# A two-layer decoder step on one core: layer 0's weight casts move from VectorE to ScalarE

## The chip, the core and the metric

One NeuronCore of a Trainium2 chip runs the whole program. Its engines are TensorE (PE in the profile; PEld is its weight load), VectorE (DVE), ScalarE (ACT), GpSimd (POOL) and SyncE (SP), whose queue issues the transfers. Each engine works off its own instructions in order. The metric is the device time of one execution in microseconds; it is the median of three runs, and lower is better.

## What is computed

```python
# layer 0: gated linear attention (GLA), 4 heads, key width 128, value width 256, chunks of 64
h = rms_norm(x, norm_gain[0])              # x: 1024 prompt rows, and 8 x 8 sample rows
u = h @ w_in                               # q, k, v, gate and a code of rank 16, in one projection
log_a = log_sigmoid(a_code @ w_up + b_a) / 16
# per chunk: b = cumsum(log_a); qd = q*exp(b); kd = k*exp(-b)
#   o = qd @ S + tril(qd @ kd^T) @ v;   S = S*exp(b_last) + (k*exp(b_last - b))^T @ v
x = x + (rms_norm(o, onorm) * silu(g)) @ w_out
# layer 1: stick-breaking attention with a paged cache for the samples, the same frame around it
```

`rms_norm(x, gain) = x * rsqrt(mean(x*x) + 1e-6) * gain`. The gain of layer 0 is not multiplied into the rows of x: it is multiplied into the rows of `w_in`, as the weights are prepared.

## The kernel before, in words

**Two-part numbers.** TensorE multiplies numbers of a reduced type (`F32R`). Each fp32 operand is held as a high part (`hi`, the number cast to that type) and a low part (`lo`, the number less its high part), and a product is three matmuls: hi·hi, hi·lo, lo·hi. So each weight tile, raw 128 x 512 in fp32 (`wr`), is prepared by `split` into `whi` and `wlo`. Layer 0's input weights are multiplied by the norm's vector (`gain`, one number for each partition) ahead of that.

**Weight tiles.** They are numbered n in the order of their use. n = 0 is the weight of the code. Then each head has four tiles for q and k (each holds two 128-row blocks, so two gains of 256 columns each) and eight for v and gate (one gain of 512 columns each): n = 1 to 12 for head 0, 13 to 24 for head 1, up to 48. From n = 49 on come weights without a gain. `place_weights` gives each tile a due time. A raw tile is fetched when the tile three before it has been split (three raw buffers), and the parts lie in a ring of ten buffers each, so a tile's parts are written when TensorE has done with the tile ten before it.

**`split` for n = 5 to 48.** VectorE multiplies the raw tile by the gain in place (L217) and casts it (L221). The low part is subtracted (L222) on VectorE where n % 3 is 2 (15 of these 44 tiles: 12 of v and gate, 3 of q and k), else on GpSimd (29 tiles). For n = 1 to 4 GpSimd multiplies (L215) and VectorE casts.

**Layer 0 by heads.** A head begins with three groups of columns of the input (c = 0, 1, 2: 384, 384 and 320 rows of x). For each, `dense_t` (L316) makes q and then k in 24 matmuls apiece; the results stand in two accumulation banks in turn. `q_out` (L497, L499) and `k_out` (L509 to L513) multiply them by the decay factors on VectorE, and so free the banks. The factors come from `decay_logits` (ScalarE L451 to L455), `decay_sums` (VectorE: xb L463, two scans L465 and L466, differences L470 and L471) and `decay_exps` (ScalarE L483 to L487). Then nine row tiles follow (`dense` L294, v and gate), with the attention of each tile (`gla_att`, `gla_state`, `gla_out`) some steps behind. The last of the nine holds the 64 sample rows; its two halves are added by `whole_rows` (ScalarE L336, then VectorE L337), and its work (L577, L578, L580, L622, L632, L635) reaches into the next head's q and k groups. This stretch, in which one head's tail and the next head's start share the engines, is called the boundary below; there are three. In head 0 the groups also hold the code (L439 to L441 take it out of its bank), and there is no older head's tail.

**What sets the order.** TensorE's order is written out by hand, as a list of times (`Timeline`). On the other engines a scheduler orders the instructions by its own simulated times when the program is built; only the gain multiplications are held in program order. A change of engine in `split` therefore moves other instructions too.

Of the kernel before, what the change touches and what calls it, by code (L numbers as in the profile page):

```python
# [13 lines left out]
AF = mybir.ActivationFunctionType  # L14
OP = mybir.AluOpType
# [61 lines left out]
def tile_hybrid_decoder(ctx, tc, x_prompt, x_sample, state_gla, cache_k, cache_v, page_table,  # L77
# [3 lines left out]
    nc = tc.nc  # L81
# [15 lines left out]
    ACT_FROM, WHI, DLO, OUT_A = 57, 6, 3, (57, 75)  # L97
# [30 lines left out]
    def sb(pool, name, shape, dtype=F32, bufs=2, tag=None):  # L128
        return pools[pool].tile(shape, dtype, name=name, tag=tag or name, bufs=bufs)
# [65 lines left out]
    def split(n, pool, engine):  # L195
        e = entries[n]
        raw, m = raws.pop(n)
        if m == NK * RANK:

            e.hi = wring.tile([128, 512], F32R, name="whi")  # L200
            nc.gpsimd.memset(e.hi.bitcast(F32), 0.0)
            x, y = (a[:, :NK * s].rearrange("p (k s) -> p k s", s=s) for a, s in ((raw, RANK), (e.hi, 48)))
            tc.keep_in_program_order(nc.vector.tensor_mul(x, x, gain[:, :NK, None].to_broadcast([128, NK, RANK])))
            nc.vector.tensor_copy(y[:, :, :RANK], x)
            nc.vector.tensor_sub(y[:, :, 32:], x, y[:, :, :RANK])
            return
        if pool is None:
            e.hi, e.lo = wring.tile([128, 512], F32R, name="whi"), wring.tile([128, 512], F32R, name="wlo")
        else:
            name, tag = pool  # L210
            e.hi, e.lo = (sb(name, f"w{i}{n}", [128, 512], F32R, 1, f"w{i}{tag}") for i in range(2))
        for s, k in e.gains:
            if 0 < n < 5:
                x = raw[:, s]
                nc.gpsimd.tensor_mul(x, x, gain[:, k:k + 1].to_broadcast(x.shape))  # L215
            else:
                tc.keep_in_program_order(nc.vector.tensor_scalar(raw[:, s], raw[:, s], gain[:, k:k + 1], None, op0=OP.mult))  # L217
        if e.first > ACT_FROM and n % 8 < WHI:
            nc.scalar.activation(e.hi[:, :m], raw[:, :m], AF.Copy)
        else:  # L220
            nc.vector.tensor_copy(e.hi[:, :m], raw[:, :m])  # L221
        engine.tensor_sub(e.lo[:, :m], raw[:, :m], e.hi[:, :m])  # L222

    def place_weights(own):

        inring, times, further = [], [], [None] * XRING
        for n, e in enumerate(entries):
            if n in own:
                pool, s = own[n]
            else:  # L230
                pool = None
                s = entries[inring[-RING]].last + 0.01 if len(inring) >= RING else e.first - (FIRST0 if n == 0 else FIRST if n < 5 else FIRST5)
                if e.first > open2 + 1 and e.last < last:
                    ends = [entries[x].last + 0.01 if x is not None else open2 + 0.01 for x in further] + [s]
                    x = ends.index(min(ends))
                    if x < XRING:
                        s, pool, further[x] = ends[x], ("at2", x), n
                if pool is None:
                    inring.append(n)
            s = max([s] + [x + 0.002 for x in times[-1:]])  # L240
            assert s < e.first - 0.05, (n, s, e.first)
            times.append(s)
            on_vector = n % 3 != 0 if OUT_A[0] < e.first < OUT_A[1] else n % 3 == 2 and DLO < e.first < 90
            at(s, split, n, pool, nc.vector if on_vector else nc.gpsimd)
            at(times[n - RAW] + 0.001 if n >= RAW else RAW0 + n * 0.01, fetch, n)
# [98 lines left out]
    gain = const.tile([128, NK], F32, name="gain")  # L344
# [318 lines left out]
    for h in range(GH):  # L663
# [3 lines left out]
        for c, (c_0, n) in enumerate(CH):  # L667
# [12 lines left out]
            for j, (key, out) in enumerate((("q", q_out), ("k", k_out))):  # L680
                lo, hi = a + (b - a) * 0.5 * j, a + (b - a) * 0.5 * (j + 1)
                dense_t(lo, hi, c_0, n, wqk,
                        lambda w, k, j=j: (w[k // 2], slice((k % 2) * 256 + j * 128, (k % 2) * 256 + j * 128 + 128)),
# [307 lines left out]
    for p in range(PAIRS):  # L991
# [27 lines left out]
        for m in range(NP // 2):  # L1019
# [20 lines left out]
            if p == PAIRS - 1:  # L1040
                st = {}
                for g in range(4):
                    n = 2 if g < 3 else 1
# [163 lines left out]
    for c, t in steps[:2 * NP - TAIL] + [(0, NP), (1, NP)] + steps[2 * NP - TAIL:]:  # L1207
# [5 lines left out]
        e = i + span  # L1213
# [41 lines left out]
```

## Time and profile before

| What | Value |
|---|---|
| median of 3 runs | 1347.07 us (1346.45 to 1347.56) |
| the profiled execution, its own time | 1348.02 us |
| its span in the profile | 1346.2 us |
| TensorE busy | 1270.1 us (94%) |
| VectorE busy | 1004.1 us (75%) |
| ScalarE busy | 719.9 us (53%) |
| GpSimd busy | 504.5 us (37%) |

The span is the time between the first and the last instruction that the profile has; the 1.8 us beside it lie before and after. Layer 0's four heads take the span's first 400 us, the output projection goes on to about 525 us, and layer 1 has the rest. A matmul's end is modelled, so TensorE's busy time overlaps from one instruction to the next; where it waits, the timeline says for what, in brackets.

### The profile page before, as it was taken

What the parts mean: (1) busy time and instruction counts of PE and PEld (TensorE: products, weight loads), DVE (VectorE), ACT (ScalarE), POOL (GpSimd) and SP (SyncE); (2) the same over time, 40 slices, a digit from 0 to 9 for tenths busy, and PEclk for the clock granted to TensorE, in tenths of its full rate; (3) what the DMA queues carried; (4) which work ended last, traced back from release to release, by engine and by line L of the source; (5) the groups of instructions that cost most, each with busy time, mean ns of one, the idle gap of its engine ahead of it and who ended that gap; (6) DMA issues with size and microseconds to landing.
All of it is one profiled execution on the core that took longest, in us unless ns stands there. A gap on an engine that the chain in (4) does not pass through costs nothing.

```text
span 1346.2 us, 23370 instructions
## 1 busy us (share of the span) xinstructions
PE 1270.1 (94%) x8025; PEld 1129.0 (84%) x8025; DVE 1004.1 (75%) x2029; ACT 719.9 (53%) x1664; POOL 504.5 (37%) x841
## 2 busy tenths in 40 slices
PE   6999999999999999989989999899998999999998
PEld 4788888888887788889989899898898988978665
DVE  7857858759565355698898988988889889896543
ACT  6446245254452135566666766667667677763221
POOL 6222323223121115363463634546446464343000
PEclk9999999999999999999999999999999999999999
DMA  6211401403337443020120200202002022134862
GB/s 199 84 43 44 135 20 55 125 20 100 122 95 236 139 136 114 20 71 26 33 74 23 71 27 28 79 23 70 28 28 77 25 76 84 33 124 153 313 207 79
DMA packets 118457, 115.80 MB, mean 86 GB/s; under 512 B 11003, under 2 KB 97923, under 8 KB 118339
## 3 DMA queue, kind: packets, MB, share of 16 engines
q1 hardware_dynamic: 118338, 114.31, 27.4%
q8 instruction: 64, 1.05, 0.3%
q14 instruction: 55, 0.44, 0.1%
HBM read 83.61 MB, written 30.67 MB: 85 GB/s over the span
## 4 chain that ended last, share of the span: by engine, by line
PE 55%; DVE 24%; ACT 8%; issue 4%; POOL 4%; DMA 3%; SPq 0%; DVEq 0%; POOLq 0%; ACTq 0%
PE acc L294 33%; PE acc L316 6%; DVE run L908 4%; PE z L882 3%; PE tr L929 2%; DVE aT L932 2%; PE o L943 2%; ACT qh L854 2%; DVE qk L811 2%; POOL rs L805 2%; DVE A L913 1%; DVE run L905 1%; DVE A L916 1%; PE o L545 1%; DVE whi L221 1%
## 5 line engine op out<-in xcount | busy, mean ns | idle before, releaser
L294 PE MATMUL acc<-whi,h 128*128 128x512 f32 (+1 forms) x1728 | 538.2, 374 | 8.5 <-DVE qk L811 6.7
L294 PEld LDWEIGHTS acc<-whi,h 128*128 128x128 f32 x1728 | 312.8, 189 | 39.7 <-ACT sh L953 3.7
L294 PE MATMUL acc<-wlo,h 128*128 128x512 f32 (+1 forms) x864 | 322.4, 373 | 1.2 <-POOL wlo L222 1.2
L316 PE MATMUL acc<-h,whi 128*128 128x256 f32 (+5 forms) x832 | 192.0, 316 | 20.4 <-DVE qk L811 10.7
L222 POOL TENSOR_TENSOR wlo<-wr,whi 128x512 fp32r<-128x512 f32 x92 | 133.2, 1451 | 132.9 <-DVE whi L221 56.5
L294 PEld LDWEIGHTS acc<-wlo,h 128*128 128x128 f32 x864 | 162.5, 188 | 18.6 <-POOL wlo L222 2.1
L316 PEld LDWEIGHTS acc<-h,whi 128*128 128x128 f32 (+2 forms) x832 | 138.6, 186 | 27.2 <-issue 10.5
L908 DVE TENSOR_TENSOR_SCAN run<-om,run 128x256 f32<-128x256 f32 x192 | 142.7, 783 | 15.9 <-ACT om L885 15.4
L931 ACT ACTIVATE aT<-tr 128x512 fp32r<-128x512 f32 (+1 forms) x160 | 88.8, 555 | 81.9 <-PE tr L929 80.0
L885 ACT ACTIVATE om<-z,bias 128x512 f32<-128x512 f32 (+1 forms) x160 | 103.0, 644 | 48.7 <-PE z L882 39.8
L316 PE MATMUL acc<-h,wlo 128*128 128x256 f32 (+2 forms) x392 | 122.9, 314 | 0.8 <-POOL wlo L222 0.8
L294 PE MATMUL acc<-w,h 128*128 128x384 f32 (+1 forms) x480 | 121.9, 365 | 0.9 <-DVE qk L811 0.9
L932 DVE TENSOR_TENSOR aT<-tr,aT 128x512 fp32r<-128x512 f32 (+1 forms) x160 | 100.8, 630 | 9.7 <-ACT aT L931 7.4
L929 PE MATMUL tr<-ident,A 128*128 128x128 f32 x576 | 90.0, 274 | 17.1 <-ACT A L886 4.8
L886 ACT ACTIVATE A<-z,bias 128x512 f32<-128x512 f32 (+1 forms) x160 | 102.3, 639 | 0.0
L943 PE MATMUL o<-aT,v 128*128 128x256 f32 (+1 forms) x640 | 98.3, 274 | 0.0
L929 PEld LDWEIGHTS tr<-ident,A 128*128 128x128 f32 x576 | 68.9, 140 | 32.8 <-ACT sq L800 9.0
L943 PEld LDWEIGHTS o<-aT,v 128*128 128x128 f32 x640 | 94.4, 188 | 1.9 <-DVE aT L932 1.2
L805 POOL TENSOR_TENSOR rs<-ms,half_exp 128x4 f32<-128x4 f32 (+1 forms) x72 | 86.7, 1204 | 19.6 <-DVE ms L803 17.1
L882 PE MATMUL z<-kc,qh 128*128 128x256 f32 x320 | 84.3, 286 | 7.1 <-DVE kc L859 7.1
L294 PEld LDWEIGHTS acc<-w,h 128*128 128x128 f32 x480 | 83.2, 189 | 6.3 <-issue 0.9
L900 POOL COPY run<-run 128x2 f32<-128x2 f32 x96 | 33.1, 345 | 134.9 <-DVE run L908 77.2
(273 smaller groups left out, 2491.7 us busy)
## 6 DMA issues: line engine op xcount, KB each, us to landing
wr<-in_w_in_b_dram SPq DMA_DIRECT2D x64, 256.0 KB, 3.0
wr<-in_w_in_a_dram SPq DMA_DIRECT2D x32, 256.0 KB, 3.1
kp<-in_cache_k_dram SPq DMA_DIRECT2D x16, 512.0 KB, 5.2
vp<-in_cache_v_dram SPq DMA_DIRECT2D x16, 512.0 KB, 5.3
o_d<-og SPq DMA_DIRECT2D x60, 128.0 KB, 1.8
x<-in_x_prompt_dram SPq DMA_DIRECT2D x8, 512.0 KB, 5.3
wr<-in_w_in_a_dram SPq DMA_DIRECT2D x32, 128.0 KB, 3.6
n<-in_state_gla_dram SPq DMA_DIRECT2D x8, 512.0 KB, 4.0
```

Source lines behind the costliest of these rows:

```text
L222: engine.tensor_sub(e.lo[:, :m], raw[:, :m], e.hi[:, :m])
L294: nc.tensor.matmul(st["ps"][:x.shape[1], :n], x, (w[k].hi if part == 0 else w[k].lo)[:, :n], start=first, stop=last)
L316: nc.tensor.matmul(st[key][:x.shape[1], :n], x, y, start=first, stop=last)
L805: nc.gpsimd.tensor_tensor(st["rs"][:n], ms[:n], half_exp[:n], op=OP.pow)
L882: nc.tensor.matmul(out, lhs, rhs, start=x == 0, stop=x == len(mm) - 1)
L885: nc.scalar.activation(u["om"][:, v0:], z[:, v0:], AF.Sigmoid, scale=-1.0, bias=K1["bias"][:, 1, hd:hd + 1])
L886: nc.scalar.activation(u["A"][:, v0:], z[:, v0:], AF.Sigmoid, bias=K1["bias"][:, 0, hd:hd + 1])
L908: nc.vector.tensor_tensor_scan(run[:, a, n - 1::-1], rev, rev, before[:, a, 0:1], op0=OP.mult, op1=OP.bypass)
L929: nc.tensor.transpose(tr[:, x], u["A"][:, col:col + 128], ident)
L931: nc.scalar.activation(hi[:, v0:], tr[:, v0:], AF.Copy)
L932: nc.vector.tensor_sub(lo[:, v0:], tr[:, v0:], hi[:, v0:])
L943: nc.tensor.matmul(q["po"][:, j, q0:], vs, part[:, x * 256 + q0:(x + 1) * 256], start=first and n == 0, stop=last and n == 3)
```

## The change

For n = 5 to 48, `split` casts on ScalarE instead of VectorE. Where the low part is VectorE's (15 tiles), the multiplication in place is gone: ScalarE multiplies by the gain as it casts (one instruction for each gain), and VectorE makes the low part in one `scalar_tensor_tensor`, raw times gain less high part. Where the low part is GpSimd's (29 tiles), VectorE still multiplies in place, then ScalarE casts, then GpSimd subtracts. The tiles n = 0 to 4 and those from 49 on are as they were.

```diff
--- before.py
+++ after.py
@@ -209,13 +209,20 @@
         else:
             name, tag = pool
             e.hi, e.lo = (sb(name, f"w{i}{n}", [128, 512], F32R, 1, f"w{i}{tag}") for i in range(2))
+        if e.gains and n >= 5 and engine is nc.vector:
+
+            for s, k in e.gains:
+                g = gain[:, k:k + 1]
+                nc.scalar.activation(e.hi[:, s], raw[:, s], AF.Copy, scale=g)
+                nc.vector.scalar_tensor_tensor(e.lo[:, s], raw[:, s], g, e.hi[:, s], op0=OP.mult, op1=OP.subtract)
+            return
         for s, k in e.gains:
             if 0 < n < 5:
                 x = raw[:, s]
                 nc.gpsimd.tensor_mul(x, x, gain[:, k:k + 1].to_broadcast(x.shape))
             else:
                 tc.keep_in_program_order(nc.vector.tensor_scalar(raw[:, s], raw[:, s], gain[:, k:k + 1], None, op0=OP.mult))
-        if e.first > ACT_FROM and n % 8 < WHI:
+        if e.gains and n >= 5 or e.first > ACT_FROM and n % 8 < WHI:
             nc.scalar.activation(e.hi[:, :m], raw[:, :m], AF.Copy)
         else:
             nc.vector.tensor_copy(e.hi[:, :m], raw[:, :m])
```

TensorE's order is the same in both programs, and from the output projection on so is that of every other engine. In the changed program all line numbers from 212 on are 7 higher (L221 is L228, L513 is L520); its L216 and L217 are the cast with the gain and the new low part, its L226 is ScalarE's plain cast.

**The boundary into head 1, VectorE**, up to the `k_out` of group 0 (the last three rows of each; x is the masked copy of the sample keys, ql a low part of q, e the decay sums). Before:

```order
L580 TENSOR_TENSOR x_1573<-kh,blk_119 128x1024
L488 COPY dec<-e_1585 128x3
L217 TENSOR_SCALAR wr<-wr,gain 128x512
L221 CAST whi<-wr 128x512
L217 TENSOR_SCALAR wr<-wr,gain 128x512
L563 TENSOR_TENSOR ql<-g,qh 128x64 x2
L652 SCALAR_TENSOR_TENSOR og<-o,rs,gt 64x256
L221 CAST whi<-wr 128x512 x2
L463 SCALAR_TENSOR_TENSOR xb<-xb,t_1616 128x320
L509 TENSOR_TENSOR g<-acc,e_1441 128x3x2x64
L512 TENSOR_TENSOR g<-acc,e_1370 128x384
L513 TENSOR_TENSOR g<-acc,e_1371 128x3x64
```

Changed:

```order
L472 SCALAR_TENSOR_TENSOR e_1515<-rst_123,xb_1460 128x384
L473 SCALAR_TENSOR_TENSOR t_1461<-rst_127,xb_1460 128x384
L570 TENSOR_TENSOR ql<-g,qh 128x64 x2
L478 TENSOR_TENSOR e_1519<-e_1515 128x192
L477 TENSOR_TENSOR e_1518<-t_1461 128x384
L217 SCALAR_TENSOR_TENSOR wlo<-wr,gain,whi 128x512
L224 TENSOR_SCALAR wr<-wr,gain 128x512
L495 COPY dec<-e_1580 128x3
L516 TENSOR_TENSOR g<-acc,e_1437 128x3x2x64
L519 TENSOR_TENSOR g<-acc,e_1367 128x384
L520 TENSOR_TENSOR g<-acc,e_1368 128x3x64
```

No cast is left ahead of `k_out`, the sample tile's og and group 2's xb went behind it, and the masked copy x went further ahead; the scans of group 1 (L472, L473), which stood well ahead of the first list's rows, now stand between it and `k_out`.

**The same boundary, ScalarE**, from the sample tile's up-copy (xr) on. Before:

```order
L336 ACTIVATE xr<-acc 64x512
L454 ACTIVATE t_1465<-t_1465 128x384
L646 ACTIVATE og,ms<-o 128x256
L455 ACTIVATE t_1465<-t_1465 128x384
L527 ACTIVATE vh<-xr 64x256 x2
L530 ACTIVATE gt<-xr 64x256
```

Changed:

```order
L343 ACTIVATE xr<-acc 64x512
L226 ACTIVATE whi<-wr 128x512 x2
L216 ACTIVATE whi<-wr,gain 128x512
L461 ACTIVATE t_1461<-t_1461 128x384
L653 ACTIVATE og,ms<-o 128x256
L534 ACTIVATE vh<-xr 64x256 x2
L537 ACTIVATE gt<-xr 64x256
```

Three casts (n = 15, 16 and 17) stand between the up-copy and what followed it.

**The end of head 0's groups, VectorE**, from the second scan of group 2 to the `q_out` of group 2 (L497 and L499; L504 and L506 in the changed program). Before:

```order
L466 SCALAR_TENSOR_TENSOR t_684<-rst_127,xb 128x320
L471 TENSOR_TENSOR e_695<-e_691 128x128
L474 TENSOR_TENSOR e_694<-e_691 128x64
L470 TENSOR_TENSOR e_694<-t_684 128x256
L488 COPY dec<-e_702 128x2
L490 COPY dec<-e_691 128x8
L497 SCALAR_TENSOR_TENSOR g<-acc,e_691 128x320
L499 SCALAR_TENSOR_TENSOR g<-acc,e_702 128x128
```

Changed:

```order
L217 SCALAR_TENSOR_TENSOR wlo<-wr,gain,whi 128x512
L224 TENSOR_SCALAR wr<-wr,gain 128x512
L478 TENSOR_TENSOR e_693<-e_689 128x128
L481 TENSOR_TENSOR e_692<-e_689 128x64
L224 TENSOR_SCALAR wr<-wr,gain 128x256 x2
L477 TENSOR_TENSOR e_692<-t_682 128x256
L495 COPY dec<-e_700 128x2
L516 TENSOR_TENSOR g<-acc,e_699 128x2x2x64
L518 TENSOR_TENSOR g<-acc,e_699 128x64
L497 COPY dec<-e_689 128x8
L504 SCALAR_TENSOR_TENSOR g<-acc,e_689 128x320
L506 SCALAR_TENSOR_TENSOR g<-acc,e_700 128x128
```

A low part, three gain multiplications and the first two instructions of `k_out` (L516, L518) came ahead of `q_out`.

**Some 10 us earlier, ScalarE**, where group 2's code is taken out of its bank (aT). Before:

```order
L487 ACTIVATE e_561<-e_561 128x192
L486 ACTIVATE e_560<-e_560 128x384
L439 ACTIVATE aT<-acc 48x320
L440 ACTIVATE aT<-acc 16x320
L451 ACTIVATE xb<-z,ba 128x320
```

Changed:

```order
L494 ACTIVATE e_559<-e_559 128x192
L493 ACTIVATE e_558<-e_558 128x384
L226 ACTIVATE whi<-wr 128x512
L446 ACTIVATE aT<-acc 48x320
L447 ACTIVATE aT<-acc 16x320
L458 ACTIVATE xb<-z,ba 128x320
```

The cast of n = 10 stands ahead of the code's two copies.

## Rows read from the trace of the kernel before

**Rows 1.** The page: busy time of each engine and its share of the span.

```profile
PE 1270.1 (94%) x8025; PEld 1129.0 (84%) x8025; DVE 1004.1 (75%) x2029; ACT 719.9 (53%) x1664; POOL 504.5 (37%) x841
```

**Rows 2.** Busy time by windows: length, PE, PEld, DVE, ACT, POOL, clock, DMA share, GB/s.

```profile
62.00:110.00 48.00, 47.43 (x246) 40.19 (x246) 28.66 (x75) 18.64 (x61) 11.10 (x18) 1.00 0.13 37
...
126.00:142.00 16.00, 14.31 (x88) 12.48 (x88) 15.87 (x34) 6.99 (x20) 7.19 (x9) 1.00 0.27 73
```

**Rows 3.** TensorE's timeline, its waits in heads 0 to 3: start, duration, [idle <-releaser].

```profile
36.99 1.04 PE L316 MATMUL acc<-h,whi 128*48 128x384 f32 x5 [0.95 <-ACT qh L562]
...
52.58 2.81 PE L316 MATMUL acc<-h,whi 128*48 128x320 f32 x18 [1.36 <-DVE g L499]
62.85 0.51 PE L294 MATMUL acc<-whi,h 128*128 128x512 f32 x1 [0.57 <-DVE g L499]
...
141.70 0.62 PE L316 MATMUL acc<-h,whi 128*128 128x384 f32 x2 [1.69 <-DVE g L513]
...
233.72 0.62 PE L316 MATMUL acc<-h,whi 128*128 128x384 f32 x2 [1.73 <-DVE g L513]
...
325.70 0.62 PE L316 MATMUL acc<-h,whi 128*128 128x384 f32 x2 [1.68 <-DVE g L513]
```

**Rows 4.** `split` by line: durations in ns, least, median and most.

```profile
L217 DVE TENSOR_SCALAR wr<-wr,gain x56: 340/474/1511, 32.3 to 337.9; 128x512 f32<-128x512 f32 x32, 128x256 f32<-128x256 f32 x24
L221 DVE CAST whi<-wr x67: 396/416/1389, 13.8 to 1180.9; 128x512 fp32r<-128x512 f32 x67
L222 POOL TENSOR_TENSOR wlo<-wr,whi x92: 1257/1338/2829, 14.3 to 1189.4; 128x512 fp32r<-128x512 f32 x92
L222 DVE TENSOR_TENSOR wlo<-wr,whi x32: 670/692/1375, 16.7 to 589.4; 128x512 fp32r<-128x512 f32 x32
L219 ACT ACTIVATE whi<-wr x20: 614/630/649, 338.1 to 524.1; 128x512 fp32r<-128x512 f32 x20
```

**Rows 5.** VectorE's scalar_tensor_tensor with both tensors in SBUF, the same way.

```profile
L463 DVE SCALAR_TENSOR_TENSOR xb<-xb,t x12: 473/546/858, 29.0 to 324.0; 128x384 f32<-128x384 f32 x8, 128x320 f32<-128x320 f32 x4
```

**Rows 6.** VectorE's timeline at the boundary into head 1.

```profile
124.80 1.51 DVE L217 TENSOR_SCALAR wr<-wr,gain 128x512 f32<-128x512 f32 x1
...
137.00 1.98 DVE L563 TENSOR_TENSOR ql<-g,qh 128x64 fp32r<-128x64 f32 x2
...
141.30 0.34 DVE L513 TENSOR_TENSOR g<-acc,e 128x192 f32<-128x192 f32 x1
```

**Rows 7.** GpSimd's timeline there.

```profile
124.68 2.79 POOL L222 TENSOR_TENSOR wlo<-wr,whi 128x512 fp32r<-128x512 f32 x2 [1.21 <-DVE whi L221]
...
137.48 1.28 POOL L222 TENSOR_TENSOR wlo<-wr,whi 128x512 fp32r<-128x512 f32 x1
```

**Rows 8.** ScalarE's timeline there.

```profile
123.31 0.59 ACT L336 ACTIVATE xr<-acc 64x512 f32<-64x512 f32 x1 [0.45 <-PE acc L294]
...
126.95 0.86 ACT L527 ACTIVATE vh<-xr 64x256 fp32r<-64x256 f32 x2 [1.72 <-DVE xr L337]
```

**Rows 9.** TensorE's timeline there: group 0's lo of n = 16, and group 1's last of q.

```profile
128.12 0.33 PE L316 MATMUL acc<-h,wlo 128*128 128x384 f32 x1
...
139.67 0.34 PE L316 MATMUL acc<-h,wlo 128*128 128x384 f32 x1
```

**Rows 10.** SP's transfers of raw tiles there, and their time to landing (least, median, most).

```profile
126.05 3.29 SPq L166 DMA_DIRECT2D wr<-in_w_in_a_dram  x3
...
DMA to landing us min/median/max: 2.7/2.8/2.9
```

**Rows 11.** Head 0, three engines: the code's copy; group 2's scan, q_out and last k matmul.

```profile
55.12 0.43 ACT L439 ACTIVATE aT<-acc 48x320 fp32r<-48x320 f32 x1 [3.14 <-PE acc L316]
...
60.29 0.80 DVE L466 TENSOR_TENSOR_SCAN t<-rst,xb 128x320 f32<-128x320 bf16 x1
...
61.97 0.31 PE L316 MATMUL acc<-h,wlo 128*128 128x320 f32 x1
...
62.51 0.28 DVE L499 SCALAR_TENSOR_TENSOR g<-acc,e 128x128 f32<-128x128 f32 x1
```

## The prediction

> **What bounds the kernel now.** I read the page first: TensorE is busy for 94% of the span, the others far less [rows 1]. So only where TensorE waits can the change gain. The table by windows shows two kinds of stretch in layer 0: in the row tiles of a head (62 to 110 us) TensorE is never short and VectorE is busy for 28.7 of 48 us; at the boundary (126 to 142) TensorE loses 1.69 us, VectorE is busy for 15.87 of 16 us and ScalarE for 7 [rows 2]. TensorE's timeline gives the waits one by one [rows 3]: 1.69, 1.73 and 1.68 us at the three boundaries, each until VectorE's L513, the last instruction of `k_out` for group 0; and in head 0 0.95, 1.36 and 0.57 us, the last two until L499, the end of `q_out`. All are waits for an accumulation bank that VectorE has to empty. The three at the boundaries make 5.10 us, the three of head 0 2.88: all that the change can win is 8 us, or 0.6%.
>
> VectorE's timeline at the boundary says why L513 is late [rows 6]: its group was complete on TensorE long before; L513 stands behind multiplications, casts and other small work, and two of these were slow, a gain multiplication at 1.51 us (median 0.474, [rows 4]) and a pair of subtractions of 64 columns each at 1.98, both while GpSimd was at a subtraction [rows 7]. So two things make VectorE late: how much it has to do, and whom it meets.
>
> **The change, part by part.** *VectorE's work.* A tile with its low part on VectorE costs 0.474 + 0.416 + 0.692 = 1.58 us now [rows 4] and one scalar_tensor_tensor afterwards. No row shows that one at 512 columns. From below it is bounded by the same operation at 384 columns, 0.546 [rows 5], from above by twice that for the most a collision cost it, 0.858 and more; I take the two-tensor subtraction of the same size, 0.69, since both read two tensors. That saves 0.89 us for each of 12 tiles, about as much for the three q and k tiles (two halves), and 0.416 for each of the 29 others: 13 + 12 = 25 us. Most of it lies where VectorE has room [rows 2] and is worth nothing.
>
> *The boundaries.* Ahead of L513 the order loses six casts (2.5 us), one gain multiplication (0.47), xb of group 2 (0.47, [rows 5]) and og of the sample tile (taken as the same), and gains the low part of n = 20 (0.69): 3.9 less 0.7 is 3.2 us. L513 ended at 141.30 + 0.34 = 141.64; it would end at 138.4. TensorE's q group 1 ends at 139.67 + 0.34 = 140.0 [rows 9], so it would find the bank empty with 1.6 us to spare. That spare time pays for what I can't place: ScalarE's casts, GpSimd in other places, a landing. Three checks. First, ScalarE: the three casts behind its up-copy (ends 123.90, [rows 8]) take 0.63 each [rows 4], to 125.8, where ScalarE now has half its time free [rows 2]; what they delay, the samples' vh, waited for VectorE's half of the up-copy until 126.95 anyhow [rows 8], and that half came after two casts and the slow multiplication that are now gone. Second, the parts of n = 15 and 16, which TensorE needs within the next microseconds: GpSimd's pair began at 124.68 and ended at 127.47, and TensorE takes the second at 128.12 [rows 7, 9]: 0.65 to spare. ScalarE's first cast ends at 123.90 + 0.6 = 124.5, when VectorE's did, so this stays as tight as it is. Third, the next raw tiles: their transfers start when GpSimd is done with a raw tile, at 126.05 now, and land 2.8 later [rows 10], at 128.9. VectorE's new order comes to that tile sooner and may wait some tenths for it. I leave 0.1 us of each wait, since one collision with a subtraction (1.34, [rows 4]) would just fit into the 1.6 and a second would not. Gain: 3 x 1.6 = 4.8 us. Bounds: 5.1 with none left, and nothing with three collisions.
>
> *Head 0, middle.* The wait of 1.36 us at 52.58 is for `q_out` of group 1. Ahead of it VectorE loses three casts and a multiplication (1.7 us) and keeps one low part; its scans then start as soon as ScalarE is ready. I take 1.2 of the 1.36; bounds 0.9 and 1.36. The 0.95 at 36.99 stays: two casts leave VectorE there, but the first low part (n = 5) now stands ahead of xb and waits for a cast that waits for its transfer.
>
> *Head 0, end: a loss.* Here the order works against the change. ScalarE's cast of n = 10 comes ahead of the code's copies, which were taken the moment TensorE had the code (55.12, [rows 11]); the decay factors of group 2 hang on that chain alone, so they are 0.5 us later (0.63 less its overlap). Behind the scan (60.29 + 0.80 = 61.09) VectorE had 2.1 us to the end of `q_out` at 62.51 + 0.28 (0.2 of it a wait for ScalarE) [rows 11]; now a low part (0.69), three multiplications (0.47 and two of 0.34, the least of [rows 4]) and the two first instructions of `k_out` (0.5, an estimate from L499's 0.28 at 128 columns for 256 and 64, [rows 11]) stand in between, 2.3 us, of which the old wait pays 0.2. So `q_out` ends 0.5 + 2.1 - 1.2 = 1.4 us later on the clock of now. It can't be much less: `k_out` can't begin before TensorE's last k matmul, at 61.97 + 0.31 = 62.28 [rows 11], and `q_out` now comes after it, so that TensorE waits at least 1.2 us in place of 0.57, whatever VectorE does. With a collision it is 2.7. I take 1.3 net for head 0, bounds 0 and 2.7.
>
> *Layer 1* has the same order on every engine and moves as a whole.
>
> Sum: -4.8 + 1.3 = -3.5 us. The profiled execution took 1348.02 us, 0.95 above the median; taken off it the sum gives 1344.5, taken off the median, which is what will be compared, 1343.6.
>
> **A rule against the change.** A cast costs 0.416 us on VectorE and 0.630 on ScalarE [rows 4], so the 44 casts take 9 us more engine time than before, on an engine that is idle for half of these stretches [rows 2]. The Trainium skill's page "ScalarE: Activation LUTs" (Rules for kernel authors) tells you to leave additions and multiplications to VectorE; the rows agree on which engine is faster. By that rule, with each boundary's three casts on the path (1.9 us), the boundaries would gain nothing (4.8 - 5.7), and the time would come out near 1349; I give that no more than a part of the last rival, since the casts replace a wait of the samples' vh.
>
> **The rivals.** *Collisions keep the boundary late.* The new low part reads two SBUF tensors, as xb and ql do, which rows 5 and 6 show to be held up while GpSimd subtracts, and ScalarE's earlier casts let more of GpSimd's subtractions run ahead of L513. For it: 1.51 and 1.98 [rows 6]. Against it: the casts and multiplications that leave can no longer be met. With two collisions L513 ends at 138.4 + 2.7 = 141.1, and 0.9 to 1.1 us of wait stay: the boundaries gain 2.2, head 0 loses 1.3, 1346.2. The Trainium skill's page "SBUF — State Buffer" (Who interferes with whom) calls it an exclusive lock between VectorE and GpSimd for the whole instruction, for a VectorE instruction with two SBUF inputs while GpSimd reads SBUF; by that rule the change takes casts and multiplications out of the lock's reach but leaves every low part in it.
>
> *Head 0 loses nothing.* If VectorE reaches the end of head 0 so early that only the wait for TensorE's last k matmul is left, its loss is 1.2 - 0.57 = 0.6, less the 1.2 of the middle; with the boundaries free in full (5.1) that is 1341.4, and with the 0.95 gone too 1340.4.
>
> *Slower: the boundary's wait stays whole and head 0 pays.* The place is VectorE's queue behind GpSimd at the boundary: three collisions more than now use up the 3.2 us that the work saves and the 1.6 of slack. The point from which it decides is L520 at 141.6 on the clock of now. Then only head 0's loss is left, up to 2.7: 1349.8. If it is slower still, ScalarE's casts are on the path as well.
>
> **How the numbers follow.** Forecast (boundaries nearly free, head 0 loses about 1.3) 0.55, own range 1342.2 to 1345.0; collisions at 1346.2 0.20; head 0 without loss 0.13; slower 0.09; something unseen 0.03. A difference of under 0.2%, 2.7 us, can hardly be told from none. The forecast lies just on the far side of it, so a quarter of its 0.55 counts as the same, with the collisions: faster 0.56, same 0.35, slower 0.09. The range for eight in ten goes from the gain without a loss to the collisions with head 0's larger loss: 1340.4 to 1347.2.
>
> **What would show it.** In the profile of the changed kernel TensorE's three waits at the boundaries (for L520 now) should be gone or a few tenths; one of a microsecond speaks for the collisions, and VectorE's low parts of over a microsecond with it. Head 0's wait near 52 should be gone and the one near 63 should be 1.2 to 3 us, still for the end of `q_out`; if it is under 0.6 I have misread the order. The plain cast on ScalarE should take 0.63, the new low part about 0.69. Waits of TensorE for a weight part (whi or wlo) of n = 15 or 16 near 127 would be new, and wrong here.

## The result, and the profile after

The changed kernel takes 1358.27 us (median of 11 runs, 1350.65 to 1361.17) against 1347.19 for the kernel before on the same chip (also 11): ratio 1.0077, 95% interval 1.0068 to 1.0086. It is 11.1 us slower where 3.6 us less were forecast. The profiled execution took 1359.6 us; its span is 1357.9, 11.7 more than before's 1346.2.

The page of the changed kernel, busy time of each engine and the granted clock in 40 slices (line numbers are now 7 higher than in the rows of before):

```profile
PE 1278.5 (94%) x8025; PEld 1134.4 (84%) x8025; DVE 986.3 (73%) x1970; ACT 747.3 (55%) x1711; POOL 516.2 (38%) x841
PEclk9889999999999999999999999999999999999999
```

Against [rows 1] VectorE lost 17.8 us of work and ScalarE took on 27.4, as meant. But TensorE is busy for 8.4 us *more* with the same 8025 products, and the second and third slice of the clock row, 9 in every slice before, show 8. TensorE's timeline, its rows with a wait of 0.3 us or more between 25 and 340 us (columns: start, us, engine, line, operation, and in brackets the wait and what ended it):

```profile
29.13 0.45 PE L323 MATMUL acc<-h,wlo 128*128 128x384 f32 x1 [0.33 <-POOL wlo L229]
36.12 0.66 PE L285 MATMUL tr<-ident,n 128*128 128x128 f32 x4 [0.92 <-DVE h L291]
40.10 1.81 PE L323 MATMUL acc<-h,whi 128*48 128x384 f32 x5 [3.33 <-ACT qh L569]
71.08 0.80 PE L301 MATMUL acc<-whi,h 128*128 128x512 f32 x1 [4.09 <-DVE g L506]
151.66 0.61 PE L323 MATMUL acc<-h,whi 128*128 128x384 f32 x2 [0.88 <-DVE g L520]
242.98 0.62 PE L323 MATMUL acc<-h,whi 128*128 128x384 f32 x2 [0.71 <-DVE g L520]
335.54 0.67 PE L323 MATMUL acc<-h,whi 128*128 128x384 f32 x2 [1.78 <-DVE g L520]
```

These answer to [rows 3]. In head 0 the wait of 0.95 is now 3.33, the one of 1.36 is gone, and that of 0.57 is 4.09; the 0.92 at 36.12, for h, is new. At the boundaries 1.69, 1.73 and 1.68 have become 0.88, 0.71 and 1.78. Following the same four products through both timelines says where the 11.7 us came in: 8.2 up to the first row tile (62.85, now 71.08), 1.7 from there to the first boundary (141.70, 151.66), 0.7 given back to the second, 0.6 more to the third, and 1.9 behind it. More than the waits can explain is in the first two and the last; the table by windows has the rest. The stretches begin about a microsecond before the first two waits end and half a microsecond after the third (columns as in [rows 2]: window, its length, busy time and instructions of each engine, PEclk, DMA share, GB/s):

```profile
39.10:45.80 6.70, 5.70 (x20) 3.47 (x21) 5.11 (x13) 3.28 (x7) 1.29 (x2) 0.50 0.09 31
69.80:76.50 6.70, 5.42 (x13) 4.28 (x14) 2.71 (x8) 0.23 (x1) 0.60 (x1) 0.50 0.46 117
336.10:339.30 3.20, 3.20 (x13) 3.20 (x12) 2.47 (x4) 1.10 (x2) 1.40 (x2) 0.50 0.67 193
```

The granted clock is 0.50, 1.2 GHz of 2.4, in all three; the kernel before had 1.00 at these places. What TensorE did there at 1.2 GHz, 5.70 + 5.42 + 3.20 = 14.3 us, would have taken half as long at 2.4: 7.2 us are lost to the clock, the larger part of the 11.7. Over all eleven runs it is about half of the loss: their mean granted clock is 0.9942, that of the kernel before 0.9983 (17 runs beside `from13`), and 0.0041 of 1357 us is 5.6 us, an estimate.

One more such stretch stands in layer 1, a microsecond or two behind a wait of TensorE of 1.75 us for qk, in both kernels (the first row is the kernel before):

```profile
528.60:532.00 3.40, 3.40 (x18) 3.27 (x18) 1.55 (x4) 2.82 (x5) 3.40 (x12) 0.52 0.31 89
540.60:544.00 3.40, 3.40 (x18) 3.40 (x18) 1.29 (x3) 2.66 (x6) 3.40 (x11) 0.53 0.07 18
```

It costs both the same and is no part of the 11.7, but it means that a half clock behind a wait could be read in the trace of before.

Why did the first wait grow? VectorE's timeline of the changed kernel, behind the second scan of group 0 of head 0:

```profile
32.22 0.93 DVE L473 TENSOR_TENSOR_SCAN t<-rst,xb 128x384 f32<-128x384 bf16 x1
34.98 0.48 DVE L224 TENSOR_SCALAR wr<-wr,gain 128x512 f32<-128x512 f32 x1 [1.83 <-DMA wr<-in_w_in_a_dram]
36.25 1.64 DVE L477 TENSOR_TENSOR e<-t 128x384 f32<-128x384 f32 x1
39.15 0.55 DVE L504 SCALAR_TENSOR_TENSOR g<-acc,e 128x384 f32<-128x384 f32 x1
39.61 0.34 DVE L506 SCALAR_TENSOR_TENSOR g<-acc,e 128x192 f32<-128x192 f32 x1
```

The multiplication is that of tile 6. In the kernel before, tile 5's multiplication stood at this place and tile 6's three microseconds later, behind e, h and tile 5's cast and low part; neither waited:

```profile
32.30 0.48 DVE L217 TENSOR_SCALAR wr<-wr,gain 128x512 f32<-128x512 f32 x1
35.63 0.48 DVE L217 TENSOR_SCALAR wr<-wr,gain 128x512 f32<-128x512 f32 x1
```

The change gives tile 5's to ScalarE; tile 6's moves up into its place, ahead of its transfer, and VectorE stands still for 1.83 us with all of e, h and `q_out` behind it. The transfer was late as well. SP's row for tile 6, before and changed:

```profile
28.97 0.54 SPq L166 DMA_DIRECT2D wr<-in_w_in_a_dram  x1
30.27 0.54 SPq L166 DMA_DIRECT2D wr<-in_w_in_a_dram  x1
```

Ahead of it in SP's queue stands the transfer of the sample rows' x, which waits for VectorE's n (L268, now L275); that ended at 28.34 before and at 29.63 here. And it landed 4.7 us after its issue, 3.7 before. Landing at 28.97 + 3.7 = 32.7, as before, it would have been there when VectorE came to it at 33.15. The late transfer alone does no harm: in `from13` (below), with head 0 in the order of before, it is issued at 30.42, and VectorE does not wait for it. In the four traces with the changed order (this one, `head0`, `vec`, `fill`) VectorE waits 1.49 to 2.09 us.

Then L477 takes 1.64 us, 0.55 before, beside a subtraction of GpSimd (36.21 to 37.48) that had come later, at 39.50, before:

```profile
36.21 1.27 POOL L229 TENSOR_TENSOR wlo<-wr,whi 128x512 fp32r<-128x512 f32 x1 [1.19 <-ACT whi L226]
```

The second wait, VectorE and GpSimd:

```profile
66.36 0.49 DVE L224 TENSOR_SCALAR wr<-wr,gain 128x512 f32<-128x512 f32 x1
67.95 1.25 DVE L495 COPY dec<-e 128x2 f32<-128x2 f32 x1
69.12 0.41 DVE L516 TENSOR_TENSOR g<-acc,e 128x256 f32<-128x256 f32 x1
69.58 0.85 DVE L497 COPY dec<-e 128x8 f32<-128x8 f32 x1
70.75 0.27 DVE L506 SCALAR_TENSOR_TENSOR g<-acc,e 128x128 f32<-128x128 f32 x1
```

```profile
67.64 2.76 POOL L229 TENSOR_TENSOR wlo<-wr,whi 128x512 fp32r<-128x512 f32 x2 [6.30 <-ACT whi L226]
```

`q_out` (its last row is L506) comes behind the queue that was forecast, and two copies of a few columns each take 1.25 and 0.85 us, together 1.8 us more than two such copies elsewhere (0.15 each), both while GpSimd is at its two subtractions (67.64 to 70.40). In `all585` (below) GpSimd subtracts nothing there, and the same two copies take 0.17 and 0.16.

At the first boundary two of VectorE's operations are stretched while GpSimd is at a subtraction (140.87 to 142.79 and 147.19 to 148.47) or at the sample tile's gt (144.87 to 147.22); xb takes 0.55 at the median of [rows 5], and the pair of ql 0.33 at the third boundary. At the second they take 1.65 and 2.11:

```profile
141.56 1.64 DVE L470 SCALAR_TENSOR_TENSOR xb<-xb,t 128x384 f32<-128x384 f32 x1
146.44 2.11 DVE L570 TENSOR_TENSOR ql<-g,qh 128x64 fp32r<-128x64 f32 x2
```

At the third boundary both things are seen once more, a wait for a transfer and a row stretched to 2.19 us (0.47 at the first boundary):

```profile
323.53 0.49 DVE L224 TENSOR_SCALAR wr<-wr,gain 128x512 f32<-128x512 f32 x1 [1.51 <-DMA wr<-in_w_in_a_dram]
332.03 2.19 DVE L224 TENSOR_SCALAR wr<-wr,gain 128x512 f32<-128x512 f32 x1
335.15 0.34 DVE L520 TENSOR_TENSOR g<-acc,e 128x192 f32<-128x192 f32 x1
```

### The profile page after: what moved, and what is told of

Read it like the earlier page. It is cut to its first block, busy times and chain, and to the rows that moved or that the text cites. A ratio compares the mean times of both kernels' runs of the same rounds, so it can differ in the third digit from the quotient of the medians.

```text
span 1357.9 us, 23394 instructions
## 1 busy us (share of the span) xinstructions
PE 1278.5 (94%) x8025; PEld 1134.4 (84%) x8025; DVE 986.3 (73%) x1970; ACT 747.3 (55%) x1711; POOL 516.2 (38%) x841
## 3 DMA queue, kind: packets, MB, share of 16 engines
q8 instruction: 64, 1.05, 0.3%
## 4 chain that ended last, share of the span: by engine, by line
PE 59%; DVE 21%; ACT 7%; issue 6%; POOL 4%; DMA 3%; SPq 0%; DVEq 0%; POOLq 0%; ACTq 0%
PE acc L301 35%; PE acc L323 8%; DVE run L915 3%; PE z L889 3%; PE tr L936 3%; DVE aT L939 2%; PE o L950 2%; ACT qh L861 2%; DVE qk L818 1%; DVE A L920 1%; POOL rs L812 1%; PE o L552 1%; DVE A L923 1%; DVE run L912 1%; PE tr L285 1%
## 5 line engine op out<-in xcount | busy, mean ns | idle before, releaser
L323 PE MATMUL acc<-h,whi 128*128 128x256 f32 (+5 forms) x832 | 195.9, 322 | 19.7 <-DVE qk L818 10.7
L229 POOL TENSOR_TENSOR wlo<-wr,whi 128x512 fp32r<-128x512 f32 x92 | 136.3, 1486 | 126.5 <-ACT whi L226 112.7
L226 ACT ACTIVATE whi<-wr 128x512 fp32r<-128x512 f32 x86 | 52.9, 629 | 65.4 <-PE acc L301 28.7
```

The source lines that it names most:

```text
L323: nc.tensor.matmul(st[key][:x.shape[1], :n], x, y, start=first, stop=last)
```

## The experiments

**Theory A**: the loss is head 0's. Without its own multiplications and casts there, VectorE's queue has other work ahead of the operations that empty TensorE's banks; two waits become 3 to 4 us; and behind such a wait TensorE runs at half clock, which costs as much again. **Theory B**: the loss is spread over layer 0; ScalarE's 47 slower casts cost something wherever they stand. Later rivals are told with their runs. All times are medians beside runs of the kernel before on the same chip, which took 1346.98 to 1347.28.

### Where: tiles 5 to 12, or the rest

`from13` makes the change for tiles 13 and later, `head0` for 5 to 12:

```diff
-        if e.gains and n >= 5 and engine is nc.vector:
+        if e.gains and n >= 13 and engine is nc.vector:         # head0: 5 <= n < 13
-        if e.gains and n >= 5 or e.first > ACT_FROM and n % 8 < WHI:
+        if e.gains and n >= 13 or e.first > ACT_FROM and n % 8 < WHI:
```

> The change for the weight tiles 13 and later alone; tiles 5 to 12 (head 0's values and gates) are split as before, and VectorE's queue in head 0 is that of before. Theory A (the loss is head 0's: VectorE's queue there is reordered by tiles 5 to 12, TensorE waits 3.3 us at 40 us and 4.1 us at 71 us, and runs at half clock behind each): neither wait nor the half-clock stretches at 40 and 71 us; the boundaries as in the changed kernel, so 1344 to 1348 us. Theory B (the loss is spread: ScalarE's 47 casts cost wherever they stand): at least three quarters of it stay, 1354 us or more.

> The change for the weight tiles 5 to 12 alone. Theory A: both long waits and both half-clock stretches of head 0 come back, 1355 to 1359 us, and the head boundaries stand as before with 1.7 us of wait each. Theory B: 8 of 47 tiles are touched, so 1347 plus a fifth of 11 us, 1349 to 1350 us.

`from13`: 1347.54 us, ratio 1.0001 (0.9991 to 1.0010). `head0`: 1356.86 us, 1.0069 (1.0054 to 1.0083), with the waits at 38.98 (3.32) and 69.50 (3.98) and a clock of 0.77 and 0.74 in the windows of 30 to 45 and 62 to 75 us. The eight tiles of head 0 make 9.7 of the 11.1 us; B, which wanted 2 to 3 for them, falls. The other 36 tiles bring nothing either: their boundaries wait 0.69, 0.75 and 1.86 us, the last with half clock behind it.

### Which half of the edit

`vec` changes only the tiles whose low part VectorE makes, `pool` only the others:

```diff
# vec
-        if e.gains and n >= 5 or e.first > ACT_FROM and n % 8 < WHI:
+        if e.first > ACT_FROM and n % 8 < WHI:
# pool
-        if e.gains and n >= 5 and engine is nc.vector:
+        if False:
-        if e.gains and n >= 5 or e.first > ...
+        if e.gains and n >= 5 and engine is not nc.vector or e.first > ...
```

> Only the tiles whose low part VectorE makes are changed (ScalarE casts with the norm's vector as scale, VectorE makes the low part in one operation); the other tiles keep VectorE's cast. Theory A: VectorE's queue in head 0 has the multiplication of tile 6 ahead of e, h and g, and tiles 12 and 13 with the key's g ahead of the query's, as in the changed kernel; the waits of 3 to 4 us are there and the time is 1354 to 1360 us. Theory B (the number of casts on ScalarE matters, and these are the smaller part): 1347 to 1351 us.

> Only the tiles whose low part GpSimd makes are changed (ScalarE casts them, VectorE still multiplies); VectorE's tiles keep its multiplication, cast and low part. Theory A: in head 0 VectorE's queue keeps the order of before at the key's and query's g, so no wait over 2 us there and 1343 to 1349 us. Theory B: 31 of 47 casts are on ScalarE, so 1354 us or more.

`vec`: 1353.21 us, 1.0046 (1.0034 to 1.0059), a little under the 1354 to 1360 that A had expected. `pool`: 1354.18 us, 1.0050 (1.0037 to 1.0063), where A had expected 1343 to 1349. TensorE's waits of `vec`, two in head 0 and the first boundary's:

```profile
39.98 1.81 PE L323 MATMUL acc<-h,whi 128*48 128x384 f32 x5 [3.27 <-ACT qh L569]
69.38 0.80 PE L301 MATMUL acc<-whi,h 128*128 128x512 f32 x1 [3.66 <-DVE g L506]
149.60 0.61 PE L323 MATMUL acc<-h,whi 128*128 128x384 f32 x2 [0.24 <-DVE g L520]
```

So `vec` has the whole of head 0's loss, and nearly the whole of the boundary's gain. `pool` is the reverse: head 0 has no wait over 1.25 us and no half clock, which A wanted, but each boundary waits 2.5 us, which A had not foreseen. `pool` at its first boundary, TensorE, two of VectorE's operations, and GpSimd:

```profile
143.25 0.62 PE L323 MATMUL acc<-h,whi 128*128 128x384 f32 x2 [2.52 <-DVE g L520]
```

```profile
134.39 2.26 DVE L587 TENSOR_TENSOR x<-kh,blk 128x1024 fp32r<-128x1024 f32 x1
139.19 1.83 DVE L473 TENSOR_TENSOR_SCAN t<-rst,xb 128x320 f32<-128x320 bf16 x1
```

```profile
134.29 1.28 POOL L229 TENSOR_TENSOR wlo<-wr,whi 128x512 fp32r<-128x512 f32 x1
137.80 2.55 POOL L229 TENSOR_TENSOR wlo<-wr,whi 128x512 fp32r<-128x512 f32 x1 [2.22 <-ACT whi L226]
```

Each of the two meets a subtraction of GpSimd and takes about a microsecond more than elsewhere (1.21 and 0.79). ScalarE's casts come at other moments than VectorE's did, so GpSimd's subtractions meet other work. Behind two of these three waits the clock fell too (0.69 in the windows 145.2 to 148.4 and 240.8 to 244.0).

### Is it the clock: work put into the waits

The changed kernel, with products that nothing reads in TensorE's queue where it waits:

```diff
+    def fill(w, n):
+        z = bank("z")
+        for _ in range(n):
+            nc.tensor.matmul(z[:, :384], w[0].hi[:, :128], H[0][:, 0, :384], start=True, stop=True)
...
                 at(hi + 0.03, out, st, h, c)
+                if h == 0 and c != 1 and key == "k":
+                    at(hi + (0.005 if c == 0 else 0.205), fill, wqk, 18 if c == 0 else 22)
```

> The changed kernel with matrix products that nothing reads (18 and 22 of 128x384, 0.17 us each at full clock) put into TensorE's queue where it waits 3.3 and 4.1 us in head 0. They make no wait shorter. Theory A1 (TensorE standing idle is what drops its clock, and each of the two half-clock stretches of 6.8 us costs 3.4 us): both stretches are gone, 1358.3 - 6.8 = 1351 to 1352 us. Rival (the time is lost to the waits alone, and the slow products behind them have another cause): 1358 us, with half clock at both places.

`fill`: 1351.21 us, 1.0037 (1.0024 to 1.0050), 7.06 less than the changed kernel. TensorE's timeline at the two places (line numbers behind L316 are 5 higher again), and the first two windows of above:

```profile
36.41 3.38 PE L320 MATMUL z<-h,whi 128*128 128x384 f32 x18
40.00 1.05 PE L328 MATMUL acc<-h,whi 128*48 128x384 f32 x5 [0.22 <-ACT qh L574]
...
64.95 3.98 PE L320 MATMUL z<-h,whi 128*128 128x384 f32 x22
68.77 0.39 PE L301 MATMUL acc<-whi,h 128*128 128x512 f32 x1
```

```profile
39.10:45.80 6.70, 6.48 (x41) 4.87 (x41) 6.18 (x14) 4.38 (x10) 2.06 (x3) 1.00 0.24 74
69.80:76.50 6.70, 6.70 (x34) 5.60 (x33) 1.40 (x5) 1.61 (x6) 0.00 (x0) 1.00 0.33 86
```

The code's first product starts at 40.00, as without the filling (40.10): the wait is as long as it was, only the clock stays at 1.00, and the five products behind it take 1.05 us in place of 1.81. That a TensorE that does useless work in a wait makes the kernel faster is what theory A says and the waits alone can't give. How much of the 7.06 is that is less sure. VectorE's order is the changed kernel's up to 42 us, so that the first place compares like with like, but behind it some of its work moved with the filling, at the second place too. Up to the first boundary the filled kernel is 5.1 us ahead (its product there starts at 146.55, not 151.66), near the 5.6 that the first two windows lost. The rest came later: the third boundary waited 0.82 us in place of 1.78 and kept its clock, and the stretch in layer 1 is missing in this execution. So the expected 1351 to 1352 was met in part by luck. The Trainium skill's page "TensorE: Matmul & The Clock Gate" (Part 1) says that the clock follows how busy the engine has lately been and halves when it was not; these rows agree.

### Is it the order: the same work in another order

The changed kernel, VectorE's low parts held to their place in the program, head 0's first tiles due 0.15 later:

```diff
-    FIRST0, FIRST, FIRST5, RAW0 = 0.9, 1.5, 6, 0.9
+    FIRST0, FIRST, FIRST5, RAW0 = 0.9, 1.5, 5.85, 0.9
...
-                nc.vector.scalar_tensor_tensor(e.lo[:, s], ...)
+                tc.keep_in_program_order(nc.vector.scalar_tensor_tensor(e.lo[:, s], ...))
```

> The changed kernel with VectorE's low parts held to their place in the program, and the first eight tiles of head 0 due 0.15 later: in VectorE's queue the multiplication of tile 6 then stands behind the query's and key's g, and those of tiles 12 and 13 behind the query's g of the last chunk; the same work is done on the same engines. Theory A (the order of VectorE's queue in head 0 makes the loss): the waits of 3.3 and 4.1 us fall to 1.4 and 0.6 or less, no half clock there, 1344 to 1348 us. Rival (more work on ScalarE and the collisions with GpSimd make VectorE late whatever the order): waits of over 2.5 us stay, 1353 us or more.

> VectorE's tiles alone, from tile 5 on, with the low parts held in place and head 0's first tiles due 0.15 later. Theory A: no long wait in head 0, boundaries as with VectorE's tiles alone: 1343 to 1346 us. Rival (head 0's casts on ScalarE delay e and q's g by themselves): the wait at 40 us stays at 2.5 us or more, 1350 us or more.

`pin585`: 1349.48 us, 1.0016 (1.0008 to 1.0025); 8.8 of the 11.1 us are back with every operation still on its engine; which of the two edits did it, the hold or the 0.15, was not tried. Of the three waits of [rows 3] in head 0 two are as before:

```profile
36.95 1.04 PE L323 MATMUL acc<-h,whi 128*48 128x384 f32 x5 [0.87 <-ACT qh L569]
63.90 0.50 PE L301 MATMUL acc<-whi,h 128*128 128x512 f32 x1 [0.57 <-DVE g L506]
```

VectorE goes from its scan (ends 33.43) through h, L478 and L477 (0.55 now) to `q_out` at 35.99 without a stop; tile 6's multiplication stands behind `k_out`, at 37.91, and waits for nothing. It is 1.5 us more than the upper end expected: the wait at 53.12 is 1.71, and the third boundary has its 1.86 with half clock behind it, as in `from13`. `vp585`, the same for `vec`, takes 1346.99 us, 1.0003 (0.9994 to 1.0012): the long waits are gone (1.27, 1.17 and 0.57) though tile 6's transfer is late here too (issued at 29.73; its multiplication stands at 37.32), but it is no faster than before, a miss of a microsecond against the 1343 to 1346 expected.

### What the boundaries can give

Four runs go from tile 13 on only, so that head 0 stays as before. `vec13` changes VectorE's tiles alone. `all13` has every tile cast with the scale on ScalarE and every low part made on VectorE (`all585`: the same from tile 5, with the two edits of `pin585`); `all13pin` holds the low parts of `all13` in place; `wide13` leaves the q and k tiles of GpSimd, two halves of 256 columns, as they are. Against the changed kernel, one of the last three lines each:

```diff
-        if e.gains and n >= 5 or e.first > ACT_FROM and n % 8 < WHI:
+        if e.first > ACT_FROM and n % 8 < WHI:
...
-        if e.gains and n >= 5 and engine is nc.vector:
+        if e.gains and n >= 13 and engine is nc.vector:                              # vec13
+        if e.gains and n >= 13:                                                      # all13
+        if e.gains and n >= 13 and (len(e.gains) == 1 or engine is nc.vector):       # wide13
```

> Only VectorE's tiles, and only from tile 13 on. Head 0 up to 60 us as before; the three head boundaries as in the run with VectorE's tiles alone, where 1.7 us of wait became 0.2 us and two of 0.3 and 0.4 us: 3 x 0.7 us less, 1344 to 1346 us. Rival (what the boundary gives is lost again behind it): 1346.5 to 1348 us.

> From tile 13 on ScalarE casts every tile with the norm's vector as scale and VectorE makes every low part in one operation of 0.73 us; GpSimd makes none of these, and VectorE multiplies none. VectorE's work for a GpSimd tile goes from 0.47 + 0.41 us to 0.73 us. Theory E (what is left of the boundary waits is VectorE's operations stretched beside GpSimd's low parts, as the 1.17, 1.49, 1.83 and 2.26 us rows of the runs before show): no stretched row there, boundary waits of 0.5 us or less in sum, 1344 to 1345.5 us. Rival (36 more operations of 0.72 us make ScalarE's queue late at the boundary): a wait of 1 us or more behind ScalarE, 1347 us or more.

> The same from tile 5 on, with the low parts held in place and head 0's first tiles due 0.15 later. Theory E: in head 0 the waits of 0.95, 1.36 and 0.57 us of before shrink too, since GpSimd's low parts there are gone: 1342.5 to 1345 us. Rival (ScalarE, which also makes h and the exponentials in head 0, becomes late): waits there as before or longer, 1346 us or more.

> The run with every low part from tile 13 on VectorE, with those held to their place in the program: VectorE's queue then has kl ahead of the three 128x256 low parts that stood before it (1.27 us), and the same work is done. Theory A (order alone): the wait of 1.68 us for kl falls to 0.3 us, no half clock behind it, and the boundaries' g is in time as without the pin: 1342.5 to 1345 us. Rival (ScalarE's casts come late and a pinned low part then holds up what stands behind it): another wait of over 1 us at the boundary, 1346.5 us or more.

> The run with VectorE's tiles alone from tile 13 on, and beside it the GpSimd tiles of values and gates (128x512) made like VectorE's; the key's and query's GpSimd tiles (two 128x256 each) stay as before. kl keeps its place ahead of them. Theory: waits of 0.3 us for kl and 0.3 us or less for g, the rows beside GpSimd's low parts less stretched: 1343 to 1345.5 us. Rival (what the boundary gives is given back behind it, as in the run with VectorE's tiles alone): 1345.5 to 1347 us.

| kernel | us | ratio (95%) | longest wait at a boundary |
|---|---|---|---|
| vec13 | 1345.87 | 0.9988 (0.9979 to 0.9996) | 0.4, behind it |
| all13 | 1348.48 | 1.0007 (0.9998 to 1.0016) | 1.69, for kl |
| all585 | 1359.09 | 1.0087 (1.0073 to 1.0100) | 1.65, for al |
| all13pin | 1353.26 | 1.0044 (1.0031 to 1.0057) | 1.64, for al |
| wide13 | 1343.55 | 0.9975 (0.9964 to 0.9986) | 0.28, for kl |

`vec13` and `wide13` came as expected, the three others did not. `all13` shows the collisions by their absence. The operations that took 2.26 and 1.83 us in `pool`, here with no subtraction of GpSimd beside them, and TensorE's new wait:

```profile
134.93 1.19 DVE L587 TENSOR_TENSOR x<-kh,blk 128x1024 fp32r<-128x1024 f32 x1
141.66 0.80 DVE L473 TENSOR_TENSOR_SCAN t<-rst,xb 128x320 f32<-128x320 bf16 x1
```

```profile
123.33 0.39 PE L552 MATMUL z<-vh,kl 128*128 128x256 f32 x1 [1.68 <-DVE kl L574]
```

The waits for g are all below 0.2, as expected, but three low parts of 256 columns (1.27 us) had come ahead of kl, which neither the theory nor its rival had, and behind the second and third wait of 1.7 us the clock fell (0.62 and 0.63 in the windows 216.4 to 219.6 and 308.6 to 311.8). `all13pin` put kl first, as expected (0.22), and lost more than it won: VectorE now stands 1.77 us at gt, behind ScalarE's queue, and the held low parts stand ahead of al; the rival of that run is what happened. `all585` failed in head 0, on ScalarE this time, where a cast waits for a transfer with h and all the exponentials behind it (ScalarE's timeline, then TensorE's):

```profile
34.57 0.72 ACT L216 ACTIVATE whi<-wr,gain 128x512 fp32r<-128x512 f32 x1 [5.25 <-DMA wr<-in_w_in_a_dram]
```

```profile
40.61 1.80 PE L323 MATMUL acc<-h,whi 128*48 128x384 f32 x5 [3.41 <-DVE g L506]
```

`wide13` beats both kernels. TensorE's only waits of over 0.2 us between 63 and 326 us are three of this kind, and the window of the boundary has it busy throughout, against 14.31 of 16 us in [rows 2]:

```profile
121.14 0.38 PE L552 MATMUL z<-vh,kl 128*128 128x256 f32 x1 [0.28 <-DVE kl L574]
```

```profile
126.00:142.00 16.00, 16.00 (x99) 14.32 (x98) 15.11 (x31) 9.84 (x26) 5.76 (x6) 1.00 0.38 111
```

## Why the prediction was wrong, point by point

**"The 0.95 at 36.99 stays": wrong, the first step that failed.** The sentence had the mechanism in hand, an operation that waits for a transfer, for tile 5, and sized it at nothing. It was tile 6 that waited, moved up in VectorE's queue and with a late transfer: 1.83 us of VectorE's time with everything behind it, and a collision added 1.1. So 0.95 became 3.33, and 0.92 for h came on top. `pin585` and `vp585` undid it by the order, with no work moved to another engine.

**Head 0's end, "1.4 us later", bounds 0 and 2.7: right place, term too small.** The queue ahead of `q_out` was the one listed, and the wait is for L506, as said. But two collisions came on top, 1.8 us on copies that the sum had not named, where the upper bound had room for one; the wait went from 0.57 to 4.09, 3.5 more. (The 2.1 us that VectorE is said to have had from the scan to the end of `q_out` are 1.7, 62.79 less 61.09; the sum does not use them.)

**Head 0's middle, 1.2 of 1.36: met, but not shown for the reason given.** That wait is gone in the changed kernel, where TensorE comes to it at half clock and behind the longer first wait. At full clock it is gone too (`fill`), with a new one of 0.61 in its place, for the code. In `pin585` and `vp585`, where the first wait is short again, it is back at 1.71 and 1.17, in another order of VectorE's.

**The boundaries, -4.8: wrong by 3.1 us.** L520 was to end at 138.4 against TensorE's 140.0. It gave back 0.81, 1.02 and -0.10 us. The rival with collisions had 0.9 to 1.1 us left, which is the first two boundaries (0.88 and 0.71); the check on the raw tiles allowed "some tenths" for a wait on a transfer, which was 0.42 us at the first and 1.51 at the third. What the sum had wrong is the spare 1.6 us, said to hold one collision: xb and ql were stretched by 1.1 and 1.8 at the first two. The gain is real all the same: `vec` brought the wait to 0.24 and `wide13` below 0.2.

**The term that was missing.** No case, not even the slower one at 1349.8, had a price for the clock, since the windows of before showed it at 1.00 throughout the heads. The stretch in layer 1 was there to be seen, at 0.98 in a window of 70 us (530 to 600) and at 0.52 close up. The premise that only where TensorE waits can time be won or lost left out how fast it runs behind a wait. The clock cost 7.2 us by the windows of the profiled execution, and `fill` gave 7.06 back, not all of it by the clock. Without the 7.2 the changed kernel would stand near 1351, slower than before and still outside the range of 1340.4 to 1347.2, for the waits of the steps above.

**Layer 1** kept its order, as said; the 1.9 us behind the third boundary are its half clock (1.6) and little else. **ScalarE's casts** as such: the plain one takes 0.632 us (0.63 forecast), the scaled one 0.715; VectorE's new low part takes 0.745 (0.69). No weight part of tiles 15 and 16 came late. ScalarE's casts were not on the path by their length, as the rule against the change had it; where they cost, as far as the traces show, it was by waiting for a transfer (`all585`) or by the moment at which they set GpSimd going (`pool`).

## What to carry to other kernels

Before taking work off an engine that runs its queue in order, look at what will move up into its place: an operation that waits for a transfer and was harmless late in the queue stops everything behind it once it stands early. Look at what starts that transfer too: here it hung on the same engine, by way of SP's queue. Price a wait of TensorE with what may follow it, not by its length alone: a wait that grows to 3 or 4 us can cost nearly twice that, and the granted clock by window shows it. When a change has a good part and a bad one, split it by place and by kind; the part that was worth making here (VectorE's tiles from 13 on, `vec13`, 0.12% less) was in the change all along, and carried on to GpSimd's wide tiles it gave 0.25% (`wide13`).

## What the runs showed of the hardware that I had not expected

- **The clock behind a wait.** Around the end of waits of 3.3 and 4.1 us TensorE's granted clock fell to 0.50 (1.2 GHz) and stayed there for 6.7 us; the same in `head0`, `vec` and, at its first wait, in `all585`. After waits of 1.68 to 2.52 us it is no matter of length alone: 1.00 behind the waits of 1.69 and 1.73 of the kernel before, 0.50 for 3.2 us behind the 1.78 of the changed kernel, a fall behind two of three waits of 2.5 us (`pool`) and two of three of 1.7 (`all13`). The wait of 1.74 to 1.76 us for qk in layer 1, which every run has, is followed by a stretch of half clock in eight of the fourteen traces and by none in six. What decides there stays open. Runs of one kernel spread with it: of the changed kernel the fastest (1350.65 us) had a mean granted clock of 0.997, the slowest (1361.17) 0.992.
- **Small copies held up by GpSimd.** A copy of 128x2 elements took 1.25 us and one of 128x8 0.85, beside GpSimd's subtractions; scans and two-tensor operations took about 1 us more in the same company; in `all585` and `all13`, without the subtractions, the same operations took their usual time. The Trainium skill's page "SBUF — State Buffer" (Who interferes with whom) tells of an exclusive lock between these two engines, held for a whole instruction, that copies and two-input operations can meet; the rows agree; that it can make a copy eight times as long as its work was new to me.
